# Layer 0's attention: the transposition of the exponentials moved from TensorE to DMA transfers through DRAM

## The chip, the cores and the metric

The kernel runs on one NeuronCore of one Trainium2 chip, in one launch. The metric is the device time of that core in microseconds. The five engines are called PE (TensorE), DVE (VectorE), ACT (ScalarE), POOL (GpSimd) and SP (SyncE, which here only issues DMA transfers); each works through its own queue of instructions in order.

## What is computed

A decoder trunk of two layers on 1024 tokens of width 1024, in float32. Layer 0 mixes tokens by attention, layer 1 by gated linear attention; each is followed by a squared-ReLU MLP. The change touches layer 0's attention alone:

```python
def dilated_attention(h, w_in, w_out):
    qkv = (h @ w_in).reshape(B, S, N_GROUPS, 3, ATTN_HEADS, HEAD_DIM)      # 3 groups, 8 heads of 128
    for g, (window, dil) in enumerate(((128, 1), (512, 4), (2048, 16))):
        q = apply_rope(qkv[:, :, g, 0], cos, sin) * (HEAD_DIM ** -0.5)
        k = apply_rope(qkv[:, :, g, 1], cos, sin)
        v = qkv[:, :, g, 2]
        ...
        s = jnp.einsum('bzhnqd,bzhnkd->bzhnqk', qr, kb)                    # per block of 128 queries
        p = jnp.exp(jnp.where(mask, s, -jnp.inf) - m)                      # m: the row's maximum
        l = jnp.sum(p, axis=-1)
        o = jnp.einsum('bzhnqk,bzhnkd->bzhnqd', p, vb) / l[..., None]
    alpha = jax.nn.softmax(lses over the groups)
    return sum(alpha * o over the groups) @ w_out
```

Queries are rows of `p`. The product with the values contracts over the keys, so the kernel needs `p` with the keys on the partitions: each 128 by 128 block of `p` has to be transposed.

## The kernel before

The work of layer 0's attention is cut into 24 units, one for each head and group (`p = 3*head + group`). Unit `p` first makes the rotated queries and keys of its head and group: 84 matmuls of 128x512 (a Strassen scheme of seven products of twelve matmuls each, line 598, into the PSUM banks pX, pY, pV, pZ). The attention of unit `p - 1` is woven into that stream. The seven products are run in the order X, Y, V, X, V, X, Z (banks), and after each half of a product a clock goes one step on, so a unit has 14 steps. A table of planned calls (`at(step, call, rank)`) says what is recorded at which step; the order in which calls are recorded is the order on every engine's queue (nothing is reordered afterwards). All DMA transfers are issued by SP's queue, in that order too.

For each pair of query blocks `j` (0 to 3) of a unit the attention does four things, and the table `POINTS` gives the step of each, counted from the start of the unit that hosts it:

- scores (`scores`, line 984): PE multiplies queries and keys into a bank pS; then `soft` (lines 998 and 1000): DVE masks and takes the minimum, ACT takes the exponential into the tile `pt` and sums it
- `turn` (lines 1011 and 1013): PE transposes the blocks into a bank pP, ACT copies them into the second half of `pt`
- `values` (line 1025): PE multiplies them with the values `v` into a bank pO; after every second `j` ACT copies pO into `orow` (line 1029) and SP stores it to DRAM (`og`)

Block counts differ by group: 15 blocks for group 0 (two key blocks for every query block but the first), 12 for group 1 (one and two in turn), 8 for group 2 (one each): 35 for a head. A step number above 14 lies in the next unit's products: step 16 is step 2 of the unit after. The last two units (the 23rd and 24th) have tables of their own (`SINGLE`, and one in `tail`).

The columns that a unit makes go through `column` (line 1078): DVE adds two parts into `c`, SP swaps its halves by two transfers into `cw` (lines 1079 and 1080), and four steps later DVE turns them into `qT` or `kT`. Columns come at steps 5, 11, 13 and 15. SP also loads weights (`raw`, line 1070, at step 3), values (`v`) and, for a head that is complete, the three groups' outputs (`rows`, line 1158), which `plan_merges` merges over the next two units.

Of the kernel before, what the change touches and what calls it, by code (L numbers as in the profile page):

```python
# [10 lines left out]
F32R = mybir.dt.float32r  # L11
BF16 = mybir.dt.bfloat16
U32 = mybir.dt.uint32
AF = mybir.ActivationFunctionType
OP = mybir.AluOpType
AX = mybir.AxisListType
# [3 lines left out]
P = 128  # L20
# [21 lines left out]
def hybrid_trunk(ctx, tc, x, norm_mix, norm_mlp, norm_fin, a_in, a_out, g_in, g_up, g_b, g_nw,  # L42
                 g_out, m_up, m_down, tab, msk, gmask, ident_d, out):
    nc = tc.nc
    pe, act, dve, pool, sp = nc.tensor, nc.scalar, nc.vector, nc.gpsimd, nc.sync
# [926 lines left out]

    scale = HD ** -0.5

    class Attention:
        def __init__(self, g, h, qT, kT):
            self.g, self.h, self.qT, self.kT, self.st = g, h, qT, kT, {}

        def scores(self, j):
            ps = bank("pS").rearrange("p (i k) -> p i k", i=2)  # L980
# [23 lines left out]
        def turn(self, j):  # L1004
# [7 lines left out]
                    n += 1  # L1012
            act.activation(tile_[:, 1, :128 * n], ps[:, :128 * n], AF.Copy)

        def values(self, j):
            tile_, row = self.st.pop(j)
            g, h = self.g, self.h
            if j % 2 == 0:
                self.po = bank("pO").rearrange("p (b d) -> p b d", d=HD)
            po = self.po  # L1020
            n = 0
            for i in range(2):
                k0, nk, _ = keys_of(g, 2 * j + i)
                for s in range(nk):
                    pe.matmul(po[:, 2 * (j % 2) + i, :], tile_[:, 1, 128 * n:128 * n + 128], self.v[:, k0 // 128 + s, :],  # L1025
                              start=(s == 0), stop=(s == nk - 1))
# [12 lines left out]

        def plan(self, c, points, turn, values):  # L1040

            def get():
                self.v = load_values(self.g, self.h)
            at(c + points[0] - 2, get)
            for j in range(4):
                t = c + points[j]
                at(t, lambda j=j: self.scores(j), 2)
                at(t + 1 + (j % 2 and points[j] == points[j - 1]), lambda j=j: self.soft(j), 2)
                at(c + turn[j], lambda j=j: self.turn(j), 3)
                at(c + values[j], lambda j=j: self.values(j), 4)  # L1050

    class Heads(Up):
# [86 lines left out]
                    self.product(p, s, range(2 * half, 2 * half + 2))  # L1139
                    advance()  # L1140

        POINTS = (8, 8, 12, 12), (12, 12, 16, 16), (16, 16, 18, 18)
        SINGLE = (8, 10, 12, 14), (12, 14, 16, 18), (14, 16, 18, 20)

        def follow(self, p, c, points):
# [105 lines left out]
    def plan_merges(h, c):  # L1251
# [10 lines left out]
            del part[half]  # L1262
            merged(h, half, merge_join(rows.pop(half), dve))
        for half in range(2):
            t = c + 9 + 11 * half
            at(t, lambda half=half: load(half))
            if half and h == HEADS - 2:
                t += 9
            at(t + 4, lambda half=half: weigh(half), 9)
            at(t + 5, lambda half=half: merge_shares(rows[half], *part[half]), 9)  # L1270
            for n in range(4):
                at(t + 6 + n, lambda half=half, n=n: merge_scale(rows[half], part[half][1], n), 9)
            at(t + 10, lambda half=half: join(half), 9)
# [1150 lines left out]
```

## Time and profile before

| what | value |
|---|---|
| median of 3 runs | 2598.63 us (2598.55 to 2598.63) |
| the profiled execution | 2597.74 us, of which 2595.9 us from the first to the last instruction |
| PE busy | 2586.4 us, 12161 matmuls |
| DVE, ACT busy | 1861.2 us (72%), 1283.6 us (49%) |
| stage of the 24 units | from 246 us to 876 us of the span |

Busy time is what an engine spent inside instructions. Matmuls are pipelined, so the busy time of one matmul is longer than the distance to the next. The chain of waits follows the work that ended last back to the start; the share of a line there is the time that the line really took from the end.

### The profile page before, as it was taken

The numbers are of one execution on the slowest core, as the hardware profiler recorded it, in microseconds if no ns is written. First come the engines' busy times: TensorE is split into PE (matmuls) and PEld (weight loads), VectorE is DVE, ScalarE is ACT, GpSimd is POOL, SyncE is SP. The second block draws the span as 40 slices with busy tenths as digits, with TensorE's granted clock in tenths as the row PEclk, the third lists the DMA queues.
The fourth block names the chain that finished last, engine by engine and source line by source line (L and its number), as shares of the span: only waits on it lengthen the run. The fifth ranks groups of instructions, "written<-read, shape, count | busy, mean of one in ns | idle before, by whom it ended". The sixth has DMA issues, their size and how long they took to land.

```text
span 2595.9 us, 33172 instructions
## 1 busy us (share of the span) xinstructions
PE 2586.4 (100%) x12161; PEld 2159.0 (83%) x12161; DVE 1861.2 (72%) x3018; ACT 1283.6 (49%) x2352; POOL 2.3 (0%) x8
## 2 busy tenths in 40 slices
PE   9999999999999999999999999999999999999998
PEld 7888888888888888888888888888888888888887
DVE  7745878888888768665657587887657866656567
ACT  6423455555556446555534345654326554553334
POOL 0000000000000000000000000000000000000000
PEclk9999999999999999999999999999999999999999
DMA  5543455565656633454775452463513444396543
GB/s 183 172 144 111 110 156 148 150 158 141 160 149 184 223 122 129 169 168 138 280 259 182 140 196 95 134 200 98 200 61 117 170 157 155 130 355 202 183 149 132
DMA packets 327029, 422.61 MB, mean 163 GB/s; under 512 B 19825, under 2 KB 192241, under 8 KB 326866
## 3 DMA queue, kind: packets, MB, share of 16 engines
q1 hardware_dynamic: 326722, 420.23, 51.1%
q8 instruction: 95, 1.56, 0.3%
q14 instruction: 68, 0.56, 0.1%
q10 hardware_dynamic: 144, 0.26, 0.0%
HBM read 279.19 MB, written 116.06 MB: 152 GB/s over the span
## 4 chain that ended last, share of the span: by engine, by line
PE 97%; DVE 2%; ACT 1%; DMA 0%; issue 0%; SPq 0%; ACTq 0%; DVEq 0%
PE pX L598 18%; PE pB L1887 13%; PE pV L598 12%; PE pA L1887 10%; PE pB L829 7%; PE pY L598 6%; PE pZ L598 6%; PE pA L829 5%; PE pd L215 3%; PE pd L213 3%; PE pd L214 3%; PE pO L1025 2%; PE pS L984 2%; PE pP L1011 1%; PE pT L334 1%; PE pB L1411 1%
## 5 line engine op out<-in xcount | busy, mean ns | idle before, releaser
L1887 PE MATMUL pB<-dh 128*128 128x512 f32 x512 | 199.4, 389 | 0.0
L1887 PE MATMUL pB<-dh,dl 128*128 128x512 f32 x512 | 199.2, 389 | 0.0
L1887 PE MATMUL pB<-dl,dh 128*128 128x512 f32 x512 | 199.2, 389 | 0.0
L222 DVE TENSOR_TENSOR dl<-sin,dh 128x1024 fp32r<-128x1024 f32 x112 | 136.6, 1220 | 45.3 <-ACT dh L219 44.7
L219 ACT ACTIVATE dh<-sin 128x1024 fp32r<-128x1024 f32 x112 | 117.9, 1053 | 90.4 <-PE pB L1887 32.7
L219 ACT ACTIVATE dh<-kept 128x1024 fp32r<-128x1024 f32 x64 | 67.9, 1061 | 182.8 <-DVE kept L1852 137.9
L598 PE MATMUL pV<-s4h,wd 128*128 128x512 f32 x448 | 150.9, 398 | 0.0
L1887 PE MATMUL pA<-dh 128*128 128x512 f32 x384 | 149.4, 389 | 0.0
L1887 PE MATMUL pA<-dl,dh 128*128 128x512 f32 x384 | 149.4, 389 | 0.0
L1887 PE MATMUL pA<-dh,dl 128*128 128x512 f32 x384 | 149.4, 389 | 0.0
L1000 ACT ACTIVATE pt<-pt,orow 128x128 f32<-128x128 f32 (+1 forms) x192 | 84.8, 442 | 95.8 <-DVE orow L998 93.7
L1887 PEld LDWEIGHTS pB<-dl,dh 128*128 128x128 f32 x512 | 96.1, 188 | 20.0
L1887 PEld LDWEIGHTS pB<-dh,dl 128*128 128x128 f32 x512 | 96.1, 188 | 19.9
L1887 PEld LDWEIGHTS pB<-dh 128*128 128x128 f32 x512 | 96.1, 188 | 19.9
L536 DVE TENSOR_TENSOR wal<-raw,wah 128x512 fp32r<-128x512 f32 x112 | 76.2, 686 | 41.0 <-ACT wah L535 41.0
L607 ACT ACTIVATE c<-c 128x512 f32<-128x512 f32 x64 | 40.4, 631 | 118.6 <-DVE c L635 77.6
L598 PEld LDWEIGHTS pV<-s4h,wd 128*128 128x128 f32 x448 | 84.1, 188 | 17.9 <-DVE rb L623 0.4
L536 DVE TENSOR_TENSOR wbl<-t,wbh 128x1024 fp32r<-128x1024 f32 x56 | 68.6, 1225 | 38.4 <-ACT wbh L535 38.4
L222 DVE TENSOR_TENSOR dl<-kept,dh 128x1024 fp32r<-128x1024 f32 x64 | 78.4, 1225 | 24.5 <-ACT dh L219 18.4
L998 DVE CUSTOM_DVE_ANT_0 pt<-pS,masks 128x128 f32<-128x128 f32 (+1 forms) x192 | 58.2, 347 | 50.8 <-PE pS L984 50.8
L598 PE MATMUL pY<-a12h,wah 128*128 128x512 f32 x224 | 89.5, 399 | 0.0
L598 PE MATMUL pZ<-a22h,wgh 128*128 128x512 f32 x224 | 89.3, 399 | 0.0
(396 smaller groups left out, 7372.8 us busy)
## 6 DMA issues: line engine op xcount, KB each, us to landing
sin<-acts SPq DMA_DIRECT2D x112, 512.0 KB, 3.8
raw<-in_mlp_w_up_dram SPq DMA_DIRECT2D x64, 512.0 KB, 6.0
acts<-s SPq DMA_DIRECT2D x64, 512.0 KB, 3.4
raw<-in_mlp_w_down_dram SPq DMA_DIRECT2D x64, 512.0 KB, 4.7
raw<-in_attn_w_in_dram SPq DMA_DIRECT2D x98, 256.0 KB, 4.4
cw<-c SPq DMA_DIRECT2D x192, 128.0 KB, 2.3
acts<-c SPq DMA_DIRECT2D x64, 256.0 KB, 2.2
kept<-in_mlp_w_down_dram SPq DMA_DIRECT2D x32, 512.0 KB, 5.8
```

Of the source, the lines that this page charges most:

```text
L213: pe.matmul(ps, sh, mh, start=start, stop=False)
L214: pe.matmul(ps, sh, ml, start=False, stop=False)
L215: pe.matmul(ps, sl, mh, start=False, stop=stop)
L219: act.activation(hi, src, AF.Copy)
L222: dve.tensor_tensor(lo, src, hi.bitcast(F32), op=OP.subtract)
L536: self.remain(lambda: dve.tensor_tensor(lo, src, hi.bitcast(F32), op=OP.subtract))
L598: pe.matmul(st[b], u[:, k, :], v, start=first and k + n == 0, stop=k == 3 and n == 2, skip_group_check=True)
L829: pe.matmul(self.acc[s][t], a[:, c], b[:, k, :], start=fresh and m + k + v == 0, stop=m == 1 and k == 1 and v == 2, skip_group_check=True)
L984: pe.matmul(ps[:, i, :128 * n], self.qT[:, 128 * b:128 * b + 128], self.kT[:, k0:k0 + 128 * n], start=True, stop=True)
L998: dve.tensor_tensor_reduce(pt[:, i, :128 * n], ps[:, i, :128 * n], masks[:, m0:m0 + 128 * n], -scale, 1e38, op0=OP.add, op1=OP.min, accum_ ...
L1000: act.activation(pt[:, i, :128 * n], pt[:, i, :128 * n], AF.Exp, scale=-1.0, bias=m, accum_out=self.row[:, r, HD:HD + 1])
L1887: pe.matmul(self.acc[s][t], a[:, k, c], b[:, k, :], start=fresh and m + k + v == 0, stop=m == 7 and k == 1 and v == 2, skip_group_check=True)
```

## The change

For the first 22 of the 24 units the transposition leaves PE. ACT copies the exponentials' 32-bit words apart into their low and their high 16-bit halves (`halves`), in rows of 128 low halves and 128 high halves of each query, and stores them from its own DMA queue to DRAM (`pscr`, eight buffers in turn). SP then issues a transposing DMA transfer of two-byte elements (`flip`) that brings them back, with the keys on the partitions and the low and high half of each query beside each other, so that the words are whole again. `values` reads the first half of `pt`, where they land. The table moves with it: halves at steps 11, 12, 15, 16; flips at 14, 15, 18, 19; values at 20, 20, 24, 24 instead of 16, 16, 18, 18. The merges of a head start four steps later (13 instead of 9). The 23rd and the 24th unit keep PE's transposes.

```diff
+    pscr = [drp.tile([2 * P * 512], U16, name=f"pscr{n}") for n in range(8)]
+    nscr = [0]
...
+        def runs(self, j):
+            n = [keys_of(self.g, 2 * j + i)[1] for i in range(2)]
+            return [(0, 2, n[0])] if n[0] == n[1] else [(0, 1, n[0]), (1, 1, n[1])]
+
+        def halves(self, j):
+            tile_, row = self.st[j]
+            scr = self.scr[j] = pscr[nscr[0] % 8]
+            nscr[0] += 1
+            words = tile_[:, 0, :].bitcast(U16).rearrange("p (i c h) -> p i h c", i=2, h=2)
+            parts = tile_[:, 1, :].bitcast(U16)
+            for b, nb, m in self.runs(j):
+                part = parts[:, 512 * b:512 * b + 256 * m * nb]
+                act.activation(part.rearrange("p (i h c) -> p i h c", i=nb, h=2),
+                               words[:, b:b + nb, :, 0:128 * m], AF.Copy)
+                act.dma_start(scr[512 * P * b:][:256 * P * nb * m].rearrange("(i p c) -> p i c", i=nb, p=P),
+                             part.rearrange("p (i c) -> p i c", i=nb))
+
+        def flip(self, j):
+            tile_, row = self.st[j]
+            scr = self.scr.pop(j)
+            out = tile_[:, 0, :].bitcast(U16)
+            n = 0
+            for b, nb, m in self.runs(j):
+                rows = 256 * nb
+                src = scr[512 * P * b:][:rows * P * m].rearrange("(r c) -> r c", c=128 * m)
+                sp.dma_start(out[:, n:n + m * rows].rearrange("p (s r) -> p s r", s=m), src, transpose=True)
+                n += m * rows
...
-                    pe.matmul(po[:, 2 * (j % 2) + i, :], tile_[:, 1, 128 * n:128 * n + 128], self.v[:, k0 // 128 + s, :],
+                    pe.matmul(po[:, 2 * (j % 2) + i, :], self.turned(j, tile_, i, s), self.v[:, k0 // 128 + s, :],
...
-                at(c + turn[j], lambda j=j: self.turn(j), 3)
+                if self.by_dma:
+                    at(c + turn[j], lambda j=j: self.halves(j), 3)
+                    at(c + flip[j], lambda j=j: self.flip(j), 3)
+                else:
+                    at(c + turn[j], lambda j=j: self.turn(j), 3)
...
-        POINTS = (8, 8, 12, 12), (12, 12, 16, 16), (16, 16, 18, 18)
+        POINTS = (8, 8, 12, 12), (11, 12, 15, 16), (20, 20, 24, 24), (14, 15, 18, 19)
...
-            t = c + 9 + 11 * half
+            t = c + 13 + 11 * half
```

How the queues stand before and after is shown on a unit of group 0 of the second head. Its four tiles of exponentials are pt_2902, pt_2922, pt_2983 and pt_3001 before, and pt_2895, pt_2913, pt_2976 and pt_2990 after.

On PE, at step 16 (between the products X and Y of the next unit) before:

```order
L598 MATMUL pX_3013<-a11h_134,wal_2892 128x512
L1011 MATMUL pP_3040<-ident_68,pt_2983 128x128 x4
L1011 MATMUL pP_3046<-ident_68,pt_3001 128x128 x4
L1025 MATMUL pO_3052<-v_2869,pt_2902 128x128 x3
L1025 MATMUL pO_3052<-v_2869,pt_2922 128x128 x4
L598 MATMUL pY_3066<-a12h_132,wah_2891 128x512
```

and at step 20 (between V and X) after:

```order
L599 MATMUL pV_3069<-s1h_536,wbl_2945 128x512
L1069 MATMUL pO_3094<-v_2862,pt_2895 128x128 x3
L1069 MATMUL pO_3094<-v_2862,pt_2913 128x128 x4
L599 MATMUL pX_3000<-s2h_617,wbh_2944 128x512
```

The transposes are gone, and the products with the values stand four steps later; nothing of the attention is left on PE between X and V.

On ACT, from step 11 to step 15 before (e3 is the copy that frees a bank of the projection, wbh and wd are weights being rounded):

```order
L535 ACTIVATE wbh_2942<-t_2927 128x1024
L1013 ACTIVATE pt_2902<-pP_2957 128x384
L1013 ACTIVATE pt_2922<-pP_2962 128x512
L1115 ACTIVATE e3_2976<-pX_2773 128x512
L1000 ACTIVATE pt_2983,orow_2984<-pt_2983,orow_2984 128x256 x2
```

and after:

```order
L1035 ACTIVATE pt_2895<-pt_2895 128x256
L1037 DMA pscr4_96<-pt_2895 128x256
L1035 ACTIVATE pt_2895<-pt_2895 128x512
L1037 DMA pscr4_96<-pt_2895 128x512
L536 ACTIVATE wbh_2944<-t_2925 128x1024
L1035 ACTIVATE pt_2913<-pt_2913 128x1024
L1037 DMA pscr5_97<-pt_2913 128x2x512
L1164 ACTIVATE e3_2969<-pX_2774 128x512
L1005 ACTIVATE pt_2976,orow_2977<-pt_2976,orow_2977 128x256 x2
L1005 ACTIVATE pt_2990,orow_2977<-pt_2990,orow_2977 128x256 x2
L1035 ACTIVATE pt_2976<-pt_2976 128x1024
L1037 DMA pscr6_98<-pt_2976 128x2x512
```

Two copies out of PSUM are replaced by copies of twice as many elements within SBUF, each followed by the issue of a store, all ahead of the copy e3 where the first pair of blocks is concerned.

On SP, from step 13 to step 19 before:

```order
L1079 DMA cw_2979<-c_2978 64x512
L1080 DMA cw_2979<-c_2978 64x512
L1079 DMA cw_3021<-c_3020 64x512
L1080 DMA cw_3021<-c_3020 64x512
L1032 DMA og1_71<-orow_2903 128x4x130
L1070 DMA raw_3075<-in_attn_w_in_dram 128x4x128 x2
L1070 DMA raw_3076<-in_attn_w_in_dram 128x4x128 x2
L1032 DMA og1_71<-orow_2984 128x4x130
L1079 DMA cw_3119<-c_3118 64x512
```

and after:

```order
L1048 DMA_TRANSPOSE pt_2895<-pscr4_96 128x1x256
L1048 DMA_TRANSPOSE pt_2895<-pscr4_96 128x2x256
L1128 DMA cw_3008<-c_3007 64x512
L1129 DMA cw_3008<-c_3007 64x512
L1048 DMA_TRANSPOSE pt_2913<-pscr5_97 128x2x512
L1119 DMA raw_3039<-in_attn_w_in_dram 128x4x128 x2
L1119 DMA raw_3040<-in_attn_w_in_dram 128x4x128 x2
L1048 DMA_TRANSPOSE pt_2976<-pscr6_98 128x2x512
L1128 DMA cw_3077<-c_3076 64x512
L1129 DMA cw_3077<-c_3076 64x512
L1048 DMA_TRANSPOSE pt_2990<-pscr7_99 128x2x512
```

The transposing transfers stand between the swaps `cw` of two columns and the loads of weights; each waits at the head of the queue for its store to have landed. The stores of the outputs `og` have moved behind the last of them. Over the 22 units there are 124 stores and 124 transposing transfers: five of each in a unit of group 0, eight in group 1, four in group 2.

More of the change, by code (lines that the diff above doesn't have):

```diff
@@ L13 @@
 U32 = mybir.dt.uint32
+U16 = mybir.dt.uint16
 AF = mybir.ActivationFunctionType
@@ L977, in __init__ @@
             self.g, self.h, self.qT, self.kT, self.st = g, h, qT, kT, {}
+            self.scr, self.by_dma = {}, False
         def scores(self, j):
@@ L1013, in turn, with same, turned @@
             act.activation(tile_[:, 1, :128 * n], ps[:, :128 * n], AF.Copy)
+        def same(self, j):
+            return keys_of(self.g, 2 * j)[1] == keys_of(self.g, 2 * j + 1)[1]
+        def runs(self, j):
[23 more added lines that the diff above has]
+                n += m * rows
+        def turned(self, j, tile_, i, s):
+            if not self.by_dma:
+                n = s + (keys_of(self.g, 2 * j)[1] if i else 0)
+                return tile_[:, 1, 128 * n:128 * n + 128]
+            m = keys_of(self.g, 2 * j)[1]
+            n = 2 * s + i if self.same(j) else s + m * i
+            return tile_[:, 0, 128 * n:128 * n + 128]
         def values(self, j):
@@ L1038, in values, with plan @@
                     sp.dma_start(to.rearrange("(p r) c -> p r c", r=8)[:, 2 * j - 2:2 * j + 2, :], row)
-        def plan(self, c, points, turn, values):
+        def plan(self, c, points, turn, values, flip=None):
+            self.by_dma = flip is not None
             def get():
```

## The prediction

> **What bounds the kernel now.** I read the page first: its busy line and the chain by engine. Then I put the attention's stage, from the first hosted unit to the last but one, into one window (columns: length, busy time of PE, of PE's weight loads, DVE, ACT and POOL with their instructions, granted clock, DMA share, GB/s).
>
> ```profile
> PE 2586.4 (100%) x12161; PEld 2159.0 (83%) x12161; DVE 1861.2 (72%) x3018; ACT 1283.6 (49%) x2352; POOL 2.3 (0%) x8
> PE 97%; DVE 2%; ACT 1%; DMA 0%; issue 0%; SPq 0%; ACTq 0%; DVEq 0%
> 285.00:850.00 565.00, 565.00 (x2989) 483.89 (x2988) 473.49 (x1006) 321.89 (x851) 0.00 (x0) 1.00 0.59 155
> ```
>
> PE is never idle in the stage (565 of 565 us), at full clock, and the chain that ends last is PE itself. So a microsecond taken from PE here is a microsecond of the end, as long as no other engine makes PE wait. The others have room: DVE is busy 84% of the stage, ACT 57%, the DMA engines 59%.
>
> **What is removed.** The chain of waits gives what the transposes (L1011) really take of the end; columns are start, length, what. The first nine rows are one stretch, with a unit of group 1; then follow the transposes of a unit of group 2 and of one of group 0.
>
> ```profile
> 617.66 1.31 PE pS L984 x8
> 618.97 0.65 PE pP L1011 x6
> 619.63 2.76 PE pZ L598 x12
> 622.38 2.73 PE pX L598 x12
> 625.11 0.72 PE pP L1011 x6
> 625.83 1.34 PE pO L1025 x12
> 627.17 2.73 PE pY L598 x12
> 629.90 1.34 PE pO L1025 x12
> 631.24 2.74 PE pV L598 x12
> ...
> 643.93 0.44 PE pP L1011 x4
> 649.87 0.44 PE pP L1011 x4
> ...
> 669.03 0.76 PE pP L1011 x7
> 675.26 0.87 PE pP L1011 x8
> ```
>
> Group 1: 0.65 + 0.72 = 1.37 us; group 2: 0.44 + 0.44 = 0.88; group 0: 0.76 + 0.87 = 1.63. Seven heads and one more unit of group 0 leave PE: 7 x 3.88 + 1.63 = **28.8 us** for 260 of the 280 transposes, 0.11 us each. The line of the instruction itself reads longer, because matmuls overlap:
>
> ```profile
> L1011 PE MATMUL pP<-ident,pt x280: 270/272/330, 284.7 to 875.9; 128*128 128x128 f32 x140
> ```
>
> By that median the saving would be 260 x 0.272 = 70.7 us. I take the chain, where consecutive starts are counted once. The dearest transposes there, 0.12 us (0.72 / 6), would make it 31.2 us; that is the best case. The products with the values cost the same wherever they stand (1.34 us behind transposes and 1.34 us behind pY).
>
> **What ACT gets.** It loses 88 copies out of PSUM and gains 124 copies within SBUF and 124 issues. The first three rows are the copies lost, the next two the nearest to those gained (copies from SBUF of 512 and 1024 elements), the last the only DMA issue of ACT's queue.
>
> ```profile
> L1013 ACT ACTIVATE pt<-pP 128x384 f32<-128x384 f32 x40 | 17.9, 484 | 17.9 <-PE pP L1011 17.3
> L1013 ACT ACTIVATE pt<-pP 128x512 f32<-128x512 f32 x24 | 13.3, 586 | 1.0 <-PE pP L1011 1.0
> L1013 ACT ACTIVATE pt<-pP 128x256 f32<-128x256 f32 x28 | 9.1, 376 | 5.3 <-PE pP L1011 5.3
> L535 ACT ACTIVATE wah<-raw 128x512 fp32r<-128x512 f32 x44 | 27.3, 620 | 0.2
> L535 ACT ACTIVATE wgh<-t 128x1024 fp32r<-128x1024 f32 x22 | 23.2, 1055 | 0.0
> L2017 ACTq DMA_DIRECT2D out_dram<-fin x1: 379/379/379, 2592.3 to 2592.3; - x1
> ```
>
> The new copies are 36 of 256 elements, 64 of 512 and 24 of 1024: 36 x 0.376 + 64 x 0.620 + 24 x 1.055 = 78.5 us, against 40.3 us x 88/92 = 38.5 us lost. The issues are 124 x 0.38 = 47 us. Together +87 us: (321.9 + 87) / (565 - 29) = 76% busy. That lies beside PE's work and I charge nothing for it. The operand is new, two-byte elements at a stride of four bytes. Below, it could be as cheap as the copies lost (no charge either); above, at double the price, ACT would be 91% busy, and the copies e1 to e5 that free PE's banks and stand behind the new work would come late (a rival below).
>
> **What SP gets.** 124 transposing issues, priced by the nearest rows, cw's.
>
> ```profile
> L1079 SPq DMA_DIRECT2D cw<-c x96: 461/464/1321, 252.4 to 854.6; - x96
> SPq L1079 <- DVE c L1078: 165.2, 39, 10.0
> ```
>
> At 0.46 us that is 57 us, and SP's queue stood 165 us in the same window only waiting for DVE's columns, so there is room. The wait for the store is the danger: behind a flip in SP's queue stand the next column's cw, the weights and og.
>
> **What the DMA engines get.** 260 blocks of 64 KB go out and come back: 17.0 + 17.0 MB beside the 87 MB of the first row here (queue, kind: packets, MB, share). The other rows are issues: KB each, and median us to landing.
>
> ```profile
> q1 hardware_dynamic: 120478, 87.00, 58.2%
> cw<-c SPq DMA_DIRECT2D x175, 128.0 KB, 2.3
> raw<-in_attn_w_in_dram SPq DMA_DIRECT2D x84, 256.0 KB, 4.6
> v<-vscr SPq DMA_DIRECT2D x16, 256.0 KB, 5.6
> oscr<-om SPq DMA_DIRECT2D x13, 256.0 KB, 2.8
> DMA to landing us min/median/max: 3.1/5.5/7.8
> ```
>
> At the same price per byte the share goes to 58 x 121/87 = 81%: room again. At more than 1.9 times that price for the new bytes the engines would be full.
>
> **The wait that is added.** PE now waits for a transfer. The tightest is the flip of j = 1 (step 15), used at step 20. In the stretch above, DVE adds the column of step 15 and SP swaps it:
>
> ```profile
> 624.52 0.68 DVE L1078 TENSOR_TENSOR c<-pZ,e 128x512 f32<-128x512 f32 x1
> 625.26 0.46 SPq L1079 DMA_DIRECT2D cw<-c  x1
> 625.77 0.60 SPq L1080 DMA_DIRECT2D cw<-c  x1
> 622.00:629.00 7.00, 7.00 (x41) 6.04 (x40) 6.86 (x18) 6.41 (x22) 0.00 (x0) 1.00 0.34 75
> ```
>
> The flip stands behind it: issued at 626.4, and its second part in group 1 at 626.9. PE, without transposes and value products between, runs pX, pY, pV from 622.38 to 622.38 + 8.20 = 630.6, and half of one pO group (0.67) before it needs j = 1: at 631.25. So the landing may take 4.35 us. The lower bound for it is cw's 2.3 us, the upper the slowest load of v, 7.8 us. Nearest is the weight load from DRAM of 256 KB: 4.6 us, though that is read with four of them in flight and the flip of step 15 runs before the weights are issued. I take 4.6: 0.25 us of waiting. I charge it to all 22 units, 5.5 us, though group 0 and 2 have one part and more time, to cover stores that ACT issues late. The flips of j = 2 and 3 share the rings with the weights of step 3 but are needed only at step 24, one pO group, pX, pS and the second pV after step 20: I charge nothing.
>
> The Trainium skill, "Advanced Engine Details and Errata", section "X-Bar Transpose (TRN2)", says that transposing DMAs are as fast as regular ones; no trace here shows one. By that rule the flip would land like a load and the sum stands. The same page, in "DGE: Hardware vs Software", calls the transposition efficiency of the hardware-generated queues, which SP and ACT use, the worse of the two. By that line the slow rival below gains.
>
> **The tail.** Merges four steps later could hold up the last head's. The trace has slack: head 6's second half is stored 8.6 us before the last rows are loaded.
>
> ```profile
> 875.66 0.36 SPq L1233 DMA_DIRECT2D oscr<-om  x1
> 884.24 0.91 SPq L1158 DMA_DIRECT2D rows<-og  x2
> ```
>
> Two steps of the tail take one block of 12 matmuls (2.73 us), so four steps are 5.5 us: covered, and within 3.1 us of not being so. Freed banks and longer-lived pt tiles I charge at nothing: PE has no wait in the stage that a bank would end, and without that cover a load of raw would wait for PE, behind SP.
>
> **The sum.** 2597.7 - 28.8 + 5.5 = 2574.4 against the profiled execution; the median is 0.9 us above that execution, so **2575 us**.
>
> **Rivals.**
> - The landings take back most of the gain (0.20). At v's median of 5.5 us the wait is 1.15 us a unit, 25 us: 2595. For it: DVE would be 473 / 536 = 88% busy, so columns and the flips behind them come later. Against: from 622 to 629 the DMA engines were 34% busy (the last row of that fence).
> - Transposing transfers are slow (0.22). At v's slowest, 7.8 us, PE waits 3.45 us in each unit: 76 us, 2646. It decides against the change from a landing of 4.35 + 28.8 / 22 = 5.7 us on, or where the new bytes cost 1.9 times the old. For it: nothing in the trace is a transposing transfer. Against: eight or nine steps lie between halves and values.
> - ACT becomes the bound (0.10): in the same stretch it is busy 6.41 of 7 us, though the merge's part of that moves four steps on; at double-price copies its lateness passes to the stores and from them to the flips. Half a microsecond to 1.5 us a unit on top of the sum gives 2586 to 2608, about 2597.
>
> That the change does not do what it says has no chance of its own: PE's removed work stands on the chain, and the clock is already 1.00.
>
> **Chances.** My forecast (2568 to 2584) has 0.48. A change of 0.2%, 5 us, is about the least that a measurement of this kernel tells from none. Of the landing rival 0.13 lies below 2593.4 and 0.07 within; of ACT's 0.03, 0.02 and 0.05 below, within and above; the slow one is above. Faster 0.64, same 0.09, slower 0.27. The range starts at the best case, 2598.6 - 31.2 = 2567, and goes to 2612, which leaves out some 0.18 of the slow rival.
>
> **What would show it.** Right: L1011 falls to 20, the chain stays PE at 97%, waits of PE for DMA pt sum to less than 10 us, flips land in under 5 us. Wrong: PE waits for pt at L1069 in each unit, or for ACT's copies; SP's queue standing at flips for their stores while cw is late; a DMA share near full.

## The result, and the profile after

| kernel | median | runs |
|---|---|---|
| before | 2598.59 us | 4 (2598.52 to 2598.63) |
| changed | 2629.16 us | 4 (2626.97 to 2630.15) |

The changed kernel is slower: ratio 1.0117, with a 95% interval of 1.0102 to 1.0131, or 30.6 us more. 2575 us was forecast, and 2612 us was the range's upper end. The profiled execution took 2626.97 us, with a span of 2625.2 us.

The page of the changed kernel first: the busy line and the chain by engine.

```profile
PE 2574.2 (98%) x11901; PEld 2140.3 (82%) x11901; DVE 1864.6 (71%) x3018; ACT 1320.7 (50%) x2388; POOL 2.3 (0%) x8
...
PE 79%; DVE 6%; DMA 6%; ACT 4%; issue 2%; SPq 1%; ACTq 1%; DVEq 0%
```

Then the waits of its PE from 285 to 900 us of the span (us in all, times, longest), its stage in one window, and the first matmul of the last unit's product Z, before and after: the same place in the work.

```profile
PE pO L1069 <- DMA pt<-pscr: 36.9, 26, 4.1
PE pS L989 <- DVE qT L1144: 2.7, 3, 1.2
```

```profile
285.00:880.00 595.00, 555.81 (x2746) 468.21 (x2745) 479.35 (x1011) 361.24 (x893) 0.00 (x0) 0.98 0.83 204
```

```profile
850.75 0.47 PE L598 MATMUL pZ<-a22h,wgh 128*128 128x512 f32 x1
878.35 0.47 PE L599 MATMUL pZ<-a22h,wgh 128*128 128x512 f32 x1
```

The 260 transposes are gone from PE, but the chain that ends last is PE for 79% instead of 97%. At the last unit's product Z the changed kernel is 27.6 us late, of the 29.3 us that the span grew by. (At the product Z of the unit ahead it is 20.2 us late, 843.5 against 823.3 us, so 7.4 us are lost in the last unit alone.) With the 28.8 us taken away, some 56 us were added by then. In the window PE stands still for 595.00 - 555.81 = 39.2 us, and its clock is 0.98 on average, which is worth another 10 us (below). The remaining 7 us or so are not assigned.

Three units in a row, one that uses values of group 0, one of group 1, one of group 2; before, then after. The first number after the stretch is its length, the second PE's busy time; the last but two is the clock.

```profile
441.80:468.50 26.70, 26.70 (x145) 22.98 (x145) 23.25 (x52) 17.27 (x48) 0.00 (x0) 1.00 0.60 159
468.50:493.30 24.80, 24.80 (x136) 21.28 (x135) 21.63 (x45) 14.38 (x40) 0.00 (x0) 1.00 0.52 134
493.30:518.70 25.40, 25.40 (x129) 21.54 (x128) 19.86 (x46) 12.67 (x32) 0.00 (x0) 1.00 0.62 161
```

```profile
444.40:473.10 28.70, 25.88 (x131) 21.59 (x130) 22.99 (x50) 17.91 (x46) 0.00 (x0) 1.00 0.90 214
473.10:501.70 28.60, 25.74 (x125) 21.64 (x125) 23.77 (x51) 18.42 (x48) 0.00 (x0) 0.94 0.83 210
501.70:525.90 24.20, 24.20 (x117) 20.44 (x117) 18.79 (x40) 13.70 (x32) 0.00 (x0) 1.00 0.74 176
```

The third stretch is shorter by 1.2 us, just the transposes that stood in it (0.44 of group 2's, 0.76 of the next group 0's). The first, less 0.87 + 0.65 of transposes, should be 25.2 us and is 28.7: 3.5 us lost. The second, less 0.72 + 0.44, should be 23.6 and is 28.6: 5.0 us lost. Neither ACT (busy 18.42 of 28.60 us) nor the set of DMA engines (0.83) is full there.

ACT's copies as a group (busy us, mean ns; idle time before them and what ended it), then the lines of the stores and of the transposing transfers (duration ns min/median/max):

```profile
L1035 ACT ACTIVATE pt<-pt 128x512 uint16<-128x512 uint16 (+2 forms) x124 | 79.4, 640 | 17.4 <-ACT pt L1035 14.0 <-DMA pt<-pscr 3.5
```

```profile
L1037 ACTq DMA_DIRECT2D pscr<-pt x124: 338/376/1659, 283.0 to 852.4; - x124
...
L1048 SPq DMA_TRANSPOSE pt<-pscr x124: 1117/1219/4771, 289.6 to 865.0; - x124
DMA to landing us min/median/max: 2.3/3.5/9.8
```

The last row belongs to the transposing transfers: they land in 3.5 us, faster than the 4.6 us that the prediction allowed. Their issue, however, holds SP's queue for 1.22 us, not 0.46. The Trainium skill, "Advanced Engine Details and Errata", section "X-Bar Transpose (TRN2)", calls transposing DMAs as fast as regular ones; for the landing the trace agrees (a plain transfer in their place below has a median of 3.5 us in one kernel, 3.8 in another), for the issue, which the page does not name apart, the row shows otherwise.

How a unit of group 1 gets late is seen on ACT. First the kernel before, from the rounding of wbh to the copy e3; the next unit starts at 468.5 us (start, length, instruction; in brackets idle time before it and what ended it).

```profile
464.51 1.04 ACT L535 ACTIVATE wbh<-t 128x1024 fp32r<-128x1024 f32 x1
465.64 0.88 ACT L1013 ACTIVATE pt<-pP 128x384 f32<-128x384 f32 x2
466.40 0.98 ACT L1178 ACTIVATE rows<-rows,me 128x128 f32<-128x128 f32 x3
467.28 0.59 ACT L1115 ACTIVATE e<-pX 128x512 f32<-128x512 f32 x1
```

The same place after; the next unit starts at 473.1 us.

```profile
469.42 0.40 ACT L1035 ACTIVATE pt<-pt 128x256 uint16<-128x256 uint16 x1
469.85 0.41 ACTq L1037 DMA_DIRECT2D pscr<-pt  x1
470.31 0.63 ACT L1035 ACTIVATE pt<-pt 128x512 uint16<-128x512 uint16 x1 [0.49 <-ACT pt L1035]
470.97 0.36 ACTq L1037 DMA_DIRECT2D pscr<-pt  x1
471.37 1.06 ACT L536 ACTIVATE wbh<-t 128x1024 fp32r<-128x1024 f32 x1 [0.44 <-ACT pt L1035]
472.34 0.40 ACT L1035 ACTIVATE pt<-pt 128x256 uint16<-128x256 uint16 x1
472.77 0.34 ACTq L1037 DMA_DIRECT2D pscr<-pt  x1
473.15 0.63 ACT L1035 ACTIVATE pt<-pt 128x512 uint16<-128x512 uint16 x1 [0.41 <-ACT pt L1035]
473.81 0.34 ACTq L1037 DMA_DIRECT2D pscr<-pt  x1
474.25 0.60 ACT L1164 ACTIVATE e<-pX 128x512 f32<-128x512 f32 x1 [0.47 <-ACT pt L1035]
```

From 469.42 to 474.25 us ACT does nothing but copies, their issues and wbh: 4.8 us for the block that took 2.8 us before. The idle time of 0.4 to 0.5 us in brackets is no wait on top of that: the issue itself, which does not count as busy, fills it but for some 0.1 us (over all 124 copies the median is 0.47 us from a copy's end to the next instruction, and 0.38 of the issue). e3 starts 1.2 us ahead of the next unit before, and 1.1 us behind its start now. What hangs on it follows in order: DVE's columns, SP's swaps, the transposing transfers behind these, and PE. First DVE's column that needs e3 and the one of step 15, then SP's queue (two transposing issues for j = 0, the swaps of that column, two issues for j = 1), then PE at j = 1:

```profile
474.89 0.69 DVE L1127 TENSOR_TENSOR c<-pX,e 128x512 f32<-128x512 f32 x1 [1.20 <-ACT e L1164]
478.11 0.69 DVE L1127 TENSOR_TENSOR c<-pZ,e 128x512 f32<-128x512 f32 x1
477.17 2.46 SPq L1048 DMA_TRANSPOSE pt<-pscr  x2
479.73 0.54 SPq L1128 DMA_DIRECT2D cw<-c  x1
480.32 0.60 SPq L1129 DMA_DIRECT2D cw<-c  x1
481.01 2.52 SPq L1048 DMA_TRANSPOSE pt<-pscr  x2
483.64 0.49 PE L1069 MATMUL pO<-v,pt 128*128 128x128 f32 x2 [1.50 <-DMA pt<-pscr]
485.48 1.10 PE L1069 MATMUL pO<-v,pt 128*128 128x128 f32 x4 [1.36 <-DMA pt<-pscr]
```

Between the two columns DVE is busy without a gap. The second one ends at 478.8 us, but SP is still in j = 0's transposing issues until 479.6. The two parts for j = 1 are then issued at 481.0 and 482.3 us, and PE waits for each. Late stores are not the reason in the changed kernel: by the trace's landing times a transposing transfer starts 4.2 us (median) behind the landing of its store, and SP stood at the head of its queue for a store only once, for 0.2 us.

### The profile page after: what moved, and what is told of

Same layout as the page of the kernel before. It is cut to its first block, busy times and chain, and to the rows that moved or that the text cites. A ratio compares the mean times of both kernels' runs of the same rounds, so it can differ in the third digit from the quotient of the medians.

```text
span 2625.2 us, 33160 instructions
## 1 busy us (share of the span) xinstructions
PE 2574.2 (98%) x11901; PEld 2140.3 (82%) x11901; DVE 1864.6 (71%) x3018; ACT 1320.7 (50%) x2388; POOL 2.3 (0%) x8
## 4 chain that ended last, share of the span: by engine, by line
PE 79%; DVE 6%; DMA 6%; ACT 4%; issue 2%; SPq 1%; ACTq 1%; DVEq 0%
PE pB L1936 13%; PE pX L599 12%; PE pA L1936 10%; PE pV L599 8%; PE pB L830 7%; PE pA L830 5%; PE pY L599 4%; PE pZ L599 4%; PE pd L216 3%; PE pd L214 3%; PE pd L215 3%; DMA cw<-c 3%; DMA pt<-pscr 2%; DMA og<-orow 1%; PE pT L335 1%
## 5 line engine op out<-in xcount | busy, mean ns | idle before, releaser
L1069 PE MATMUL pO<-v,pt 128*128 128x128 f32 x560 | 80.6, 286 | 37.2 <-DMA pt<-pscr 36.9
L1069 PEld LDWEIGHTS pO<-v,pt 128*128 128x128 f32 x560 | 73.8, 195 | 46.4 <-DMA pt<-pscr 41.7
L599 PE MATMUL pX<-s2h,wbh 128*128 128x512 f32 x224 | 92.2, 411 | 0.0
```

The lines of the kernel that those rows point to most:

```text
L599: pe.matmul(st[b], u[:, k, :], v, start=first and k + n == 0, stop=k == 3 and n == 2, skip_group_check=True)
L1069: pe.matmul(po[:, 2 * (j % 2) + i, :], self.turned(j, tile_, i, s), self.v[:, k0 // 128 + s, :], start=(s == 0), stop=(s == nk - 1))
```

## The experiments

Two theories went in. SP: the transposing issues, at 1.22 us, hold up everything behind them in SP's queue. ACT: the copies and stores hold up e3 and with it the columns. Rivals were the landing itself, and the price of the moved table. Two figures in the expectations are misread: the waits for a copy's end are the issues themselves (above) and must not be added to them, and the 44.6 us of waits at the products with the values are 36.9 us on PE. Each median stands against a kernel before at 2598.1 to 2598.6 us on the same chip.

### One part at a time

**table_only**: the moved steps with PE's transposes.

```diff
-            self.by_dma = flip is not None
+            self.by_dma = False
```

> Only the table of steps is the changed one (values four steps later, turns at 11, 12, 15, 16, merges four steps later); the transposes stay on PE. Both theories: PE has the same work as before and no transfer to wait for, so 2598 to 2601 us, no wait at the products with the values, and 280 transposes on PE. If the move itself delays something (the last head's merges above all, where the changed kernel lost about 9 us), it is 2603 to 2608 us and the loss stands behind 850 us of the span.

Measured: 2603.91 us, ratio 1.0020 (1.0011 to 1.0030). The table alone costs 5.4 us; 2.5 us of it are one wait of PE in the last unit, for merged outputs that are loaded for the output projection (ol).

```profile
PE pT L260 <- DMA ol<-oscr: 2.5, 1, 2.5
```

**g2_only**: a second table `KEPT` with the old steps; `flip` is given to units of group 2 alone.

```diff
-                self.follow(p - 1, 14 * p, self.POINTS if p < self.count - 1 else self.SINGLE)
+                self.follow(p - 1, 14 * p, self.SINGLE if p == self.count - 1 else
+                            self.POINTS if (p - 1) % NG in (2,) else self.KEPT)
...
+        KEPT = (8, 8, 12, 12), (12, 12, 16, 16), (16, 16, 18, 18)
```

> Only the seven units of group 2 use the transfers (four stores and four transposing transfers each); groups 0 and 1 keep PE's transposes at their old steps. In the changed kernel group 2 showed waits of 0.0 to 0.1 us a unit, so both theories (SP's transposing issues of 1.22 us push the swaps and flips back; ACT's copies and stores push the copy e3 and with it the columns back) expect the full saving of 7 x 0.88 = 6.2 us here: 2592 to 2593 us, waits at the products with the values under 1 us in all, no stretch at half clock. If the loss sat in the tail or in the merges alone, 2597 to 2603 us.

Measured: 2595.02 us, ratio 0.9985 (0.9976 to 0.9995). The transfers pay in group 2; PE waits for them once, 0.4 us, and another 2.5 us once for qT. Of the 6.2 us expected 3.5 are there; part of table_only's loss may be the rest.

**g1_only**: the same with `in (1,)`.

> The changed kernel's transfers in the seven units of group 1 alone; groups 0 and 2 keep PE's transposes at their old steps. In the changed kernel these units took about 28.0 us from start to start, in the kernel before 24.8. If the loss is made inside a unit of group 1 (eight copies, stores and transposing transfers each), it shows here too: 7 x 3.2 = 22 us, about 2619 to 2623 us. If group 0's unit ahead hands its lateness on, group 1 alone waits little: 2598.6 - 7 x 1.37 = 2589, and some 3 us more for the tail: 2589 to 2596 us.

Measured: 2625.78 us, ratio 1.0105 (1.0088 to 1.0122): with seven units of group 1 alone the kernel loses 27.5 us, of 30.6 with all 22, without help from group 0. (The moved merges are in both.) The three stretches of g1_only, as above:

```profile
448.60:474.70 26.10, 26.10 (x140) 22.39 (x140) 21.10 (x45) 16.22 (x44) 0.00 (x0) 1.00 0.66 183
474.70:504.90 30.20, 27.35 (x129) 22.96 (x128) 24.72 (x60) 18.54 (x51) 0.00 (x0) 0.89 0.76 175
504.90:530.30 25.40, 25.40 (x128) 21.54 (x127) 19.19 (x38) 12.03 (x30) 0.00 (x0) 1.00 0.48 125
```

The DMA share over the stage is 0.63 here, against 0.59 before, so a full set of DMA engines is not the cause.

### One cost taken away, in all 22 units

**plain_back**: no transposition on the way back. (This kernel, plain_hi and no_split compute something else than the reference.)

```diff
-                act.activation(part.rearrange("p (i h c) -> p i h c", i=nb, h=2),
+                act.activation(part.rearrange("p (i c h) -> p i h c", i=nb, h=2),
...
-                src = scr[512 * P * b:][:rows * P * m].rearrange("(r c) -> r c", c=128 * m)
-                sp.dma_start(out[:, n:n + m * rows].rearrange("p (s r) -> p s r", s=m), src, transpose=True)
+                src = scr[512 * P * b:][:rows * P * m].rearrange("(p r) -> p r", p=P)
+                sp.dma_start(out[:, n:n + m * rows], src)
```

> The transfers back into pt are plain instead of transposing (same bytes, same place in SP's queue, and ACT's copies keep the words whole, with the same strides on the read side); the blocks are not transposed, so this computes something else. SP theory: the issue falls from 1.22 to about 0.46 us, 151 us of SP's queue to 57 us; the waits at the products with the values fall from 44.6 us to under 12 us, half-clock stretches vanish, 2573 to 2585 us. ACT theory: stores, copies and columns are as late as in the changed kernel, the waits stay above 30 us, 2610 us or more. If the landing of a transposing transfer were the cost, not its issue, the landing would fall from 3.5 us to under 2.9 us and the time lie between, about 2600 us.

Measured: 2622.63 us, ratio 1.0087 (1.0072 to 1.0102). It looked like a verdict against the SP theory, but the copies had become dearer, because their output is strided too (median 775 ns against 618):

```profile
L1035 ACT ACTIVATE pt<-pt x124: 472/775/1377, 282.1 to 846.8; 128x512 uint16<-128x512 uint16 x64, 128x256 uint16<-128x256 uint16 x36, 128x1024 uint16<-128x1024 uint16 x24
L1048 SPq DMA_DIRECT2D pt<-pscr x124: 332/462/1707, 289.6 to 857.7; - x124
```

**plain_hi**: the same at the old price of the copies.

```diff
-                               words[:, b:b + nb, :, 0:128 * m], AF.Copy)
+                               words[:, b:b + nb, 1:2, 0:128 * m].to_broadcast([P, nb, 2, 128 * m]), AF.Copy)
```

> Plain transfers back instead of transposing ones, as in plain_back, but ACT's copies write their output in rows again, at the changed kernel's own price (0.62 us for 512 elements; in plain_back they took 0.78): they copy the high half twice, so this computes something else. If the price of SP's transposing issues (151 against about 57 us) has a part of its own in the loss, it now shows without the dearer copies: 2605 to 2616 us, waits of PE for qT as in the changed kernel (2.7 us). If the issue's price counts for little, 2619 us or more, as plain_back.

Measured: 2609.20 us, ratio 1.0041 (1.0026 to 1.0056), with copies at 618 ns and issues at 512 ns. So the issue's price is worth about 20 us; the landing did not get shorter (3.8 us). PE's waits for qT did not stay at 2.7 us, as expected, but were 12.0.

**no_split**: no copies on ACT, and a constant is stored.

```diff
-                act.activation(part.rearrange("p (i h c) -> p i h c", i=nb, h=2),
-                               words[:, b:b + nb, :, 0:128 * m], AF.Copy)
-                act.dma_start(scr[512 * P * b:][:256 * P * nb * m].rearrange("(i p c) -> p i c", i=nb, p=P),
-                             part.rearrange("p (i c) -> p i c", i=nb))
+                act.dma_start(scr[512 * P * b:][:256 * P * nb * m].rearrange("(k p w) -> p k w", k=nb * m, p=P),
+                             ident.bitcast(U16)[:, None, :].to_broadcast([P, nb * m, 256]))
```

> ACT's 124 copies are left out; its 124 stores write a constant of the same size instead (so the products use other data), and no store waits for a copy's end. The transposing transfers are all there. SP theory: flips still take 151 us of SP's queue, so the waits at the products with the values stay above 25 us and the time above 2605 us. ACT theory: with 78.5 us of copies and about 14 us of waits for their ends gone, e3 and the columns come in time, the waits fall under 12 us, 2573 to 2588 us.

Measured: 2602.04 us, ratio 1.0011 (1.0002 to 1.0021), with the transposing issues still at 1.24 us (median). ACT's copies are worth 27 us, with the issues of the stores still there. The waits at the products with the values fell by half only, to 17.7 us.

**one_each**: the three blocks of an uneven pair lie side by side, and each pair has one copy, one store, one transfer.

```diff
-            return [(0, 2, n[0])] if n[0] == n[1] else [(0, 1, n[0]), (1, 1, n[1])]
+            return [(0, 2, n[0])] if n[0] == n[1] else [(0, 3, 1)]
...
+                at_ = 128 if self.by_dma and not i and not self.same(j) else 0
+                to = pt[:, i, at_:at_ + 128 * n]
...
+                if nb == 3:
+                    src = tile_[:, 0, :].bitcast(U16)[:, 256:1024].rearrange("p (i c h) -> p i h c", i=3, h=2)
```

> Each pair of query blocks gets one copy, one store and one transposing transfer, the uneven pairs too (their three blocks lie side by side): 88 of each instead of 124, the 36 saved all in units of group 0 and 1. ACT loses about 7 us of copies, 14 us of issues and 15 us of waits for a copy's end, SP 36 x 1.22 = 44 us. ACT theory, by no_split's 27 us for 92 us of ACT's time: 2615 to 2619 us; more, to 2605 us, if the units of group 1 hold the loss, since 28 of the 36 are theirs. If only the landings count (3.5 us, unchanged), no change: 2626 to 2630 us.

Measured: 2599.82 us, ratio 1.0008 (0.9999 to 1.0018), more than either reading allowed: 29 us back for 36 fewer of each, 28 of them in group 1. The elements copied and the bytes moved are the same, so these 29 us go by the number of copies, stores and issues.

### The order on the queues

**flip_first** (rank 0 instead of 3 for `flip`, ahead of the column) and **later** (two more steps):

```diff
-                    at(c + flip[j], lambda j=j: self.flip(j), 3)
+                    at(c + flip[j], lambda j=j: self.flip(j), 0)
```

> In each step the transposing transfers are issued ahead of the column's swaps cw instead of behind them; nothing else moves. If PE waits because the transfers stand behind cw, which waits for DVE's column and that for ACT's e3, the waits at the products with the values fall from 44.6 us to under 20 us and the time to 2600 to 2612 us. If the stores themselves come late from ACT, or SP's queue as a whole is the limit, nothing is won: 2624 us or more, with the waits of PE for qT (2.7 us) growing, since cw now stands behind the transfers.

```diff
-        POINTS = (8, 8, 12, 12), (11, 12, 15, 16), (20, 20, 24, 24), (14, 15, 18, 19)
+        POINTS = (8, 8, 12, 12), (11, 12, 15, 16), (22, 22, 26, 26), (14, 15, 18, 19)
...
-            t = c + 13 + 11 * half
+            t = c + 15 + 11 * half
...
-                t += 9
+                t += 7
```

> Values at steps 22, 22, 26, 26 instead of 20, 20, 24, 24, and the merges two steps later; halves and transposing transfers stand where they stood. If the loss is lateness (a chain of queues that is 1 to 4 us too long, without any queue being full), two steps more, 2.7 us, take most of the waits: under 12 us at the products with the values, half-clock stretches gone, 2585 to 2600 us. If a queue is full (ACT or SP), the lateness grows until it is met: the waits stay above 30 us and the time above 2618 us.

Measured: flip_first 2647.14 us (1.0189, 1.0174 to 1.0205), later 2648.83 us (1.0193, 1.0177 to 1.0208). Both are worse than the changed kernel. In flip_first the swaps now stand behind the transfers and DVE waits for them, twice as long as in the changed kernel (flip_first, then the changed kernel):

```profile
DVE cw L1136 <- DMA cw<-c: 48.8, 22, 5.7
DVE cw L1136 <- DMA cw<-c: 24.9, 23, 2.6
```

In later the waits at the products with the values are gone from the stage, but PE now waits for the copies e, which free the bank pX, and longer for qT:

```profile
PE pX L599 <- ACT e L1164: 30.8, 10, 5.2
PE pS L989 <- DVE qT L1144: 18.6, 11, 4.7
```

At one of these waits (5.2 us, up to 406.5 us of the span) e starts at 405.85 us, behind two copies and two stores; the first of the stores is issued 1.8 us after its copy has ended, while transposing transfers are under way. More time between store and use did not help: PE meets ACT's lateness at the next place. What held that store stays open.

### ACT or SP, in group 1 alone

g1_only has two copies, two stores and two transposing transfers for each pair. **g1_one** takes one of each, **g1_one_flip** two copies and stores with one transfer, **g1_one_copy** one copy and store with two transfers; all with the blocks side by side. The lines that differ:

```diff
# g1_one_flip, in halves
+            for b, e in ((0, 1), (1, 3)):
+                act.activation(parts[:, b:e], words[:, b:e], AF.Copy)
+                act.dma_start(scr[0:768 * P].rearrange("(b p c) -> p b c", b=3, p=P)[:, b:e],
+                              tile_[:, 1, :].bitcast(U16)[:, 0:768].rearrange("p (b c) -> p b c", b=3)[:, b:e])
# g1_one_copy, in flip
+            for b, e in ((0, 256), (256, 768)):
+                sp.dma_start(out[:, b:e].rearrange("p (s r) -> p s r", s=1), src[b:e], transpose=True)
```

> g1_only with one copy, one store and one transposing transfer for each pair of blocks instead of two of each (four in a unit instead of eight), on the way of one_each. Both theories: most of the 27 us of g1_only goes. By the waits that group 1 showed in one_each (0.8 to 1.7 us a unit, 8 us) and the saving of 7 x 1.37 = 9.6 us, with some 3 us for the tail and 3 for half clock: 2598 to 2606 us. The next two runs take this step by halves.

> g1_only with one transposing transfer for each pair instead of two; copies and stores stay two each. SP is relieved of four issues a unit, 4 x 1.22 = 4.9 us, ACT of nothing. SP theory: 2600 to 2610 us. ACT theory (e3, columns and stores late behind the copies): 2618 us or more.

> g1_only with one copy and one store for each pair instead of two; the transposing transfers stay two each. ACT is relieved of about 4 x (0.20 + 0.38 + 0.43) = 4.0 us a unit, SP of nothing. ACT theory: 2600 to 2610 us. SP theory: 2618 us or more. If both halves of the step win alike, the two queues stand one behind the other in the same chain of waits.

| kernel | copies and stores a pair | transfers back a pair | median | ratio (95%) |
|---|---|---|---|---|
| g1_only | 2 | 2 | 2625.78 us | 1.0105 (1.0088 to 1.0122) |
| g1_one_flip | 2 | 1 | 2623.90 us | 1.0099 (1.0084 to 1.0114) |
| g1_one_copy | 1 | 2 | 2612.78 us | 1.0060 (1.0043 to 1.0077) |
| g1_one | 1 | 1 | 2611.01 us | 1.0047 (1.0032 to 1.0062) |

Half the copies and stores win 13.0 us, half the transfers 1.9 us. In group 1 it is ACT's copies and stores. In which units the 20 us of plain_hi lie, which made all 124 issues cheaper, was not taken apart. What stays open is g1_one itself, still 12.9 us above the kernel before; the moved table (5.4 us in table_only) may be a part.

### The merges' place

In the unit shown above, the first half's join (two sums on DVE, from 466.3 to 467.8 us) stands ahead of the masks, for whose exponentials ACT waits before its copies. **merge_moved** puts the merges into the unit after (`t = c + 24 + 9 * half`, two scalings a step, for heads 0 to 5); **one_merge** does so on top of one_tail below.

> The changed kernel with the merges of all heads but 6 and 7 moved out of the unit that hosts group 1: first half weighed at step 0 of the next unit (hosting group 2) and joined at step 4, second half weighed at step 9 and joined at step 13; two scaling steps in one. In the changed kernel the first half's join (two sums, 1.3 us on DVE) stands right ahead of group 1's masks, and its 12 scalings on ACT ahead of the exponentials. If this place makes ACT's copies and stores late in group 1: its waits fall from 1.0 to 4.5 us a unit to under 1.5 us, 2605 to 2617 us. If the copies and stores alone are the cause, no change: 2624 to 2634 us.

> one_tail (one copy, one store and one transposing transfer a pair, old tail) with the merges moved as in merge_moved. If the merges' place is part of the cause, the 17 us of waits that one_tail showed at the products with the values fall under 8 us: 2584 to 2591 us, better than one_g02's 2591.3. If not: 2594 to 2598 us.

Measured: 2673.39 us (1.0289, 1.0272 to 1.0306) and 2632.83 us (1.0133, 1.0118 to 1.0148), a clear miss. In one_merge the waits of group 1's values vanished from one unit (470.2 to 498.3 us), but PE waited there for qT, and group 2 waited for its values in the unit after (498.3 to 527.2 us). The rows of the two stretches, in this order:

```profile
PE pS L989 <- DVE qT L1149: 2.6, 1, 2.6
...
PE pO L1074 <- DMA pt<-pscr: 2.9, 1, 2.9
```

The place of the merges does decide where PE waits, but the new place is worse. One cause is seen in merge_moved's waits: DVE stood 6.4 us, six times, at the column's tile `c` for the store of `om`. Whether a third place would be better was not tried.

### A version that beats both

**one_tail** is one_each with the 21st and 22nd unit and head 6's merges at the old steps, **one_g02** the same without group 1, **g02_rows** with the first load of `rows` two steps earlier, **one_pool** is one_tail with copies and stores on POOL and its queue.

```diff
# one_tail (one_g02: (0, 2))
+                            self.POINTS if p < 21 and (p - 1) % NG in (0, 1, 2) else self.KEPT)
+            t = c + (9 if h == HEADS - 2 else 13) + 11 * half
# g02_rows
+            at(t if half or h == HEADS - 2 else t - 2, lambda half=half: load(half))
# one_pool
+                pool.tensor_copy(part.rearrange("p (i h c) -> p i h c", i=nb, h=2), src)
+                pool.dma_start(scr[512 * P * b:][:256 * P * nb * m].rearrange("(i p c) -> p i c", i=nb, p=P),
```

> one_each, but the 21st and 22nd unit keep PE's transposes at their old steps, and head 6 merges at its old steps, so that the tail is that of the kernel before. In one_each PE waited 6.2 us in the last unit, and the table alone cost about 3 us behind it. If these are the tail's own price: 2599.8 - 9.2 + 0.88 + 1.63 = 2593 us. If something else becomes last there, 2597 to 2600 us.

> one_tail with group 1 back on PE's transposes: seven units of group 0 and six of group 2 use the transfers. Saving 7 x 1.63 + 6 x 0.88 = 16.7 us; with the waits that group 0 showed in one_each (0.8 to 1.0 us a unit) 2588 us. If group 1's queues caused these too, 2582 us; if group 0's waits grow, 2592 us or more.

> one_g02 with the first load of a head's rows (786 KB) two steps earlier, so that it no longer runs beside group 0's transposing transfers (one of them landed 6.0 us after its issue in one_each, with that load and the weights in flight). If the landing behind that load makes group 0's waits (9.6 us in one_g02): under 4 us, 2584 to 2588 us. If they come from ACT or from SP's order, no change: 2590 to 2593 us.

> one_tail with the copies and the stores on POOL and its queue (88 each), where they stand in front of nothing else; ACT keeps only its work of the kernel before, less the copies out of PSUM. ACT theory: e3 and the columns come in time, waits of PE fall under 5 us, 2574 to 2586 us. If POOL's copy of two-byte elements is slow, or its stores land late (more than 4 us behind ACT's), the transfers back stand at SP's head for them and the time is above 2600 us.

| kernel | median | ratio (95%) |
|---|---|---|
| one_tail | 2595.45 us | 0.9989 (0.9979 to 0.9998) |
| one_g02 | 2591.30 us | 0.9976 (0.9967 to 0.9986) |
| g02_rows | 2591.39 us | 0.9973 (0.9963 to 0.9983) |
| one_pool | 2604.23 us | 1.0023 (1.0013 to 1.0032) |

one_g02 beats both kernels, by 7.0 us against before. g02_rows shows that the load of `rows` beside group 0's transfers is not what makes them late. one_pool is the miss: ACT is free (285.6 us busy in the stage, one_tail 350.3), but DVE's time for about the same work grows from 477.4 to 516.1 us, and PE waits 11.7 us for qT. The stage in one window, of one_pool and then of one_tail (the third busy time is DVE's, the fourth ACT's, the fifth POOL's), and PE's waits for qT in one_pool:

```profile
285.00:850.00 565.00, 541.21 (x2727) 457.40 (x2726) 516.11 (x996) 285.60 (x765) 142.35 (x157) 1.00 0.86 207
```

```profile
285.00:850.00 565.00, 548.34 (x2768) 463.82 (x2767) 477.40 (x1012) 350.34 (x857) 0.00 (x0) 1.00 0.86 210
```

```profile
PE pS L989 <- DVE qT L1149: 11.7, 7, 2.1
```

## Why the prediction was wrong, step by step

- **What is removed** was right: the stretch without waits is shorter by the 1.2 us that the chain gave for its transposes, and g2_only is faster.
- **What ACT gets** had the sizes right and the charge wrong; this is the step that failed. The copies took 79.4 us (78.5 forecast), an issue 0.376 us (0.38). They were charged at nothing, because ACT would be 76% busy. But four copies and four issues stand in order ahead of e3, within two steps: 3.5 of the 4.8 us shown. The stretch shown before the forecast had ACT busy 6.41 of 7 us, and that row was used for a rival of 0.10 only. That rival, ACT as the bound, came nearest, but its condition, copies at double price, did not come true, and its lateness was to pass through the stores, which were in time; it passed through e3. It was priced at half a microsecond to 1.5 us a unit on top of the sum; the units shown lost 3.5 and 5.0 us. Leaving the copies out (no_split) gives 27 us back, and in group 1 half the copies and stores 13.0 us.
- **What SP gets** took the issue's price from cw's row, 0.46 us. Measured: 1.22 us, 151 us instead of 57. No row of before held a transposing issue, and no upper end was given. plain_hi puts this at 20 us. The danger that the prediction named, SP standing at a flip for its store, did not come (0.2 us in all).
- **What the DMA engines get** was right: share 0.83 against 81% forecast.
- **The wait that is added** was placed wrongly. The landing was better than assumed (3.5 us, not 4.6). The issue was assumed where the kernel before would have let it stand, 4.0 us behind the start of the unit and 4.5 for the second part. In the unit shown it stands 481.0 - 473.1 = 7.9 us behind, and 9.2 for the second part. DVE's column of that step starts 5.0 us behind the unit's start, not 624.52 - 622.38 = 2.1: 2.9 us of the delay, behind e3. The rest, 1.0 us and 1.8 for the second part, is the transposing issues in SP's queue. The margin was reckoned with ACT, DVE and SP at their old times, though all three are links of it.
- **The tail**, charged at nothing, costs: table_only is 5.4 us above before (in its profiled execution 2.7 us gather up to the last unit's beginning, and 3.4 come there and behind it), and one_each's last unit gains 4.4 us when it keeps its old steps (one_tail), net of the 2.5 us of transposes that return.
- **The clock** was not in the sum at all; it is worth about 10 us of the profiled execution (below).

no_split's 27.1 us, plain_hi's 20.0 and table_only's 5.4 make 52.5 of the 54 us between forecast and result. Taking single links out of one chain need not add up, so this is no division, and the near agreement may be chance. That the links are in one chain is read from the unit shown; the runs that only move work along it (flip_first, later and merge_moved, all worse) fit it.

## What to carry to other kernels

Work that is taken off the engine on the critical path is paid for in the order of the queues that take it, not in their busy share: look at what stands behind each new instruction, within the one or two steps in which it falls, and at what it waits for itself. Where an engine copies and then issues a transfer of the copy, both stand in its queue (0.63 and 0.38 us here): count them as one piece, and make few large pieces; here 88 instead of 124 took back 29 of 31 us with the same bytes. And make such a change by parts: group 2 gains from it by itself (3.5 us), groups 0 and 2 together with one copy a pair (7.0 us), and group 1 loses in every form tried.

## What the runs showed of the hardware

- A transposing transfer held SP's queue for 1.22 us at its issue, a plain one in its place 0.46 to 0.51; they landed in 3.5 us, and in 3.5 and 3.8 us (medians).
- A two-byte copy on ACT with strided input and contiguous output took 0.63 us for 512 elements, a four-byte copy of as many 0.62; with strided output as well the median rose from 618 to 775 ns.
- PE's clock halves behind waits. Three stretches of the changed kernel, the first with the two waits for the parts of j = 1, the second right behind it, the third a little later:

```profile
482.24:485.65 3.41, 0.66 (x3) 0.47 (x4) 2.82 (x5) 2.93 (x8) 0.00 (x0) 1.00 0.56 138
485.65:489.06 3.41, 3.41 (x11) 2.83 (x12) 3.38 (x5) 3.41 (x12) 0.00 (x0) 0.50 1.12 297
489.60:493.00 3.40, 3.40 (x21) 2.92 (x20) 2.28 (x8) 2.00 (x6) 0.00 (x0) 1.00 0.77 147
```

PE is busy throughout the second and the third, but runs 11 matmuls in one and 21 in the other: waits of 2.9 us in all cost another (1 - 0.50) x 3.41 = 1.7 us. The trace has five such stretches in the stage, four of 3.41 us and one of twice that, 20.5 us in all: 10 us lost. The Trainium skill, "TensorE: Matmul & The Clock Gate", Part 1, describes half clock after an idle window of about 3.4 us, in windows that run freely; the trace agrees on the length, but the window need not be idle. Counted in steps of 3.41 us from the start of one of them, every window of the stage in which PE was busy for 1.44 us or less is followed by half clock, and none of 1.65 us or more. That fits g1_one, where PE stood 1.9 us in a unit at clock 1.00.
- POOL's two-byte copies (1.1 to 1.2 us for 768 to 1024 elements) slowed DVE: 39 us more busy time in the stage. DVE's sums `t` (line 574, 0.69 us) took 1.32 us on average where such a copy ran beside them.
